# Two-layer hybrid encoder: weight splits leave GpSimd, native tiles read the residual itself

## Chip, cores and metric

The kernel runs on one core of one Trainium2 chip. The metric is device time in microseconds (us) of one execution; lower is better. The engines are TensorE (PE in the profile, its weight loads PEld), VectorE (DVE), ScalarE (ACT), GpSimd (POOL) and SyncE (SP, which issues the DMAs).

## The reference

Two layers run over 592 tokens at once: 16 meta tokens, 512 prompt tokens and 64 tokens of a running stream; the model width is 1024. Everything is float32.

```python
for l in range(2):
    h = h + 0.5 * swiglu(rms(h, ln_ffa_w[l]), wg, wu, wd)    # 1024 -> 2816 -> 1024
    h = h + mixer(rms(h, ln_mix_w[l]))                       # Mamba-2 SSD heads and HGRN2 heads
    h = h + 0.5 * swiglu(rms(h, ln_ffb_w[l]), wg, wu, wd)
y = rms(h, ln_f_w)
# rms(x, w) = x * rsqrt(mean(x * x) + 1e-6) * w      swiglu(x) = (silu(x @ wg) * (x @ wu)) @ wd
```

So there are four feed-forward blocks with the same shapes, and two mixers. Each block reads 34.6 MB of weights, once.

## The kernel before

The residual `h` is kept transposed in SBUF: 8 tiles (`m` or `k`) of 128 features by 592 tokens, worked on as two halves of 296 tokens.

**Split products.** Most products are made of float32r parts: a weight is rounded to a high part `wh` (float32r) and the rest is the low part `wl`; the activation likewise (`gh`, `gl` or `qh`, `ql`). Three products are summed: high by high, high by low, low by high (L578 to L580, and L607 to L609 in a quad). `convert` makes the parts of one weight unit of 128 x (4 x 128): the high part (L518 on ScalarE or L520 on GpSimd), then the low part (L524, on VectorE or GpSimd).

**A feed-forward block** has 22 tiles of 128 hidden features. The first two (`NPLAIN`, the native ones) are multiplied as plain float32 (`job.whole`, L571). They do not wait for the norm's statistics: the input is `h` times the norm's weight, in a tile `nh` made by `Norm.parts`, and the result is multiplied by the reciprocal root mean square `rstd` afterwards, in the sinks `gate` and `up` (L919 to L944). While TensorE runs these four jobs (two gates, two ups), the statistics become ready and `Norm.combine` builds the normed input of the remaining 20 tiles: for each of 4 `j` a pair `x1`, `x2` (L762), sums and differences of its halves in `y` and `x1` (L764 to L766), one more combination after the first split (L773), and `split` makes the parts `qh` (ScalarE, L792) and `ql` (VectorE, L794) of four combinations `p`.

**A quad** is one of the 20 tiles: gate and up together as seven multiplications of half-size blocks (a Strassen-like scheme), each of 4 x 3 products, 84 in all. Its weights need four sums (`combine`, L502) of the four raw tiles, and seven conversions. The sinks of the seven multiplications evict partial sums (ScalarE L858, L864, L868; VectorE L872 to L891); three of the multiplications start only after the eviction of an earlier one (`gates`), since they add to the same sum. `u` is one of these evicted sums (L864 on ScalarE, L877 on VectorE).

**Down products** follow after 6, 6, 5 and 5 tiles and add to `h` (L964). The mixer projects with the same split products, and runs its scans on all engines.

**Buffers.** `bT` holds 50 tiles of 592 columns, `braw` 6 raw weight tiles, `bhi` and `blo` 6 high and 6 low parts, `bzq` 4 tiles that the weight sums use.

**Order.** Every chain is a generator that yields (engine, duration, what it waits for, buffers it needs). `Plan.run` simulates time, always takes the task with the earliest start, then the lowest rank, and the instructions are issued in that order; each engine executes its own in that order. The rank is mostly the place of the job in the list of jobs (`near(order)`). Where a task names two engines, the planner takes the one that ends first by its cost formulas. `hops` are the costs it adds for handing over.

```python
        t = yield (S, G), (ns_act(n), 700 + 0.95 * n), (*waits, prev) if prev else waits, (bhi,)
        ...
        t = yield (V, G), (ns_dve(n), ns_pool(n)), (t,), (blo,)
```

`chain` makes the high parts take their buffers in the order of the jobs. Raw weight tiles are fetched in the order of the jobs by one generator (`fetch`), as `braw` has room; a native tile keeps its raw buffers until its second half has been multiplied.

Of the kernel before, what the change touches and what calls it, by code (L numbers as in the profile page):

```python
# [9 lines left out]
F32 = mybir.dt.float32  # L10
# [104 lines left out]
def ns_dve(n):  # L115
    return 157 + n / 0.96


def ns_act(n):
    return 205 + n / 1.2  # L120
# [6 lines left out]
class Plan:  # L127
    def __init__(self, hops):

        self.hops = hops  # L130
        self.tasks, self.busy, self.seq = [], {}, 0
# [10 lines left out]
    def start(self, req, behind):  # L142
# [49 lines left out]
def body(ctx: ExitStack, tc: tile.TileContext, a: dict, o: dict):  # L192
# [7 lines left out]
    plan = Plan({PE: (200.0, 60.0), V: (130.0, 0.0), S: (150.0, 0.0), G: (100.0, 0.0)})  # L200
# [199 lines left out]
    class Job:  # L400
# [5 lines left out]
        def __init__(self, name, src, ks, x, ev, hvs, sink, rank=1, few=0, after=None, whole=False, late=False):  # L406
# [37 lines left out]
    def fetch():  # L444
# [9 lines left out]
        for i, job in enumerate(jobs):  # L454
# [4 lines left out]
            for k0, k1, u in job.units:  # L459
                t = yield "DMA", 190 * (k1 - k0), (), (braw,)  # L460
# [3 lines left out]
                if job.whole:  # L464
                    u.hi = raw
                    u.ready.set(t)
                elif job.few:
# [3 lines left out]
                if i == 0:  # L471
                    for b, g in ((0, 1), (1, 1), (2, 1)) if k0 == 0 else ():
                        yield from fetch_x(b, g)
            if i == 1:
# [5 lines left out]
                load_params()  # L480

# [25 lines left out]
    def convert(u, raw, chain, done, *waits):  # L507
# [4 lines left out]
        t = yield (S, G), (ns_act(n), 700 + 0.95 * n), (*waits, prev) if prev else waits, (bhi,)  # L512
# [4 lines left out]
        if plan.pick == 0:  # L517
            S.activation(hi, raw, AF.Copy)  # L518
        else:
            G.tensor_scalar(hi, raw, 1.0, 0.0, op0=ALU.mult, op1=ALU.add)  # L520
# [20 lines left out]
    def products():  # L541
# [12 lines left out]
        for job, hv, ks in steps:  # L554
# [29 lines left out]
            if hf == job.hvs[-1][0]:  # L584
                if job.whole:
                    braw.put(t, len(job.units))
                else:
                    bhi.put(t, len(job.units))
# [85 lines left out]
    class Norm:  # L674

        def __init__(self, key, l, name, whole=False):
# [1242 lines left out]
```

## Time and profile before

| | us |
|---|---|
| median of 3 runs | 2409.16 (2406.61 to 2411.24) |
| the profiled execution | 2411.44 |
| its span, first to last instruction | 2409.7 |
| TensorE busy | 2333.8 |
| VectorE busy | 1747.8 |
| ScalarE busy | 980.6 |
| GpSimd busy | 627.7 |

The profile is of one execution. Busy times are unions of intervals; matmuls overlap in the pipeline, so their listed durations are longer than the time from one to the next. The next VectorE or ScalarE instruction also starts shortly before the listed end of the one ahead of it. The granted clock is 1.00 at 2.4 GHz and 0.50 at 1.2 GHz, as a mean over the stretch.

### The profile page before, as it was taken

The numbers are of one execution on the slowest core, as the hardware profiler recorded it, in microseconds if no ns is written. First come the engines' busy times: TensorE is split into PE (matmuls) and PEld (weight loads), VectorE is DVE, ScalarE is ACT, GpSimd is POOL, SyncE is SP. The second block draws the span as 40 slices with busy tenths as digits, with TensorE's granted clock in tenths as the row PEclk, the third lists the DMA queues.
The fourth block names the chain that finished last, engine by engine and source line by source line (L and its number), as shares of the span: only waits on it lengthen the run. The fifth ranks groups of instructions, "written<-read, shape, count | busy, mean of one in ns | idle before, by whom it ended". The sixth has DMA issues, their size and how long they took to land. (4 is left out here: it accounts for less than half of the span.)

```text
span 2409.7 us, 43335 instructions
## 1 busy us (share of the span) xinstructions
PE 2333.8 (97%) x16703; PEld 2262.8 (94%) x16703; DVE 1747.8 (73%) x3130; ACT 980.6 (41%) x1987; POOL 627.7 (26%) x630
## 2 busy tenths in 40 slices
PE   7999999999999899999989999999999998999998
PEld 6899999998889799999979999999988997999998
DVE  6866667687986776676677667676889768685775
ACT  5434334334444443343544344352353543353443
POOL 4322212243422223121222212123334114110012
PEclk9899999999999999999999999999999999999999
DMA  4222332331112123323222332323311122323232
GB/s 127 75 84 88 89 92 78 95 83 44 39 47 74 53 80 88 90 80 94 80 70 79 88 88 82 90 83 89 80 50 36 51 62 70 96 85 92 80 99 73
DMA packets 370366, 188.27 MB, mean 78 GB/s; under 512 B 16672, under 2 KB 367696, under 8 KB 370160
## 3 DMA queue, kind: packets, MB, share of 16 engines
q1 hardware_dynamic: 370160, 185.50, 26.9%
q8 instruction: 132, 2.16, 0.4%
q14 instruction: 74, 0.61, 0.1%
HBM read 180.94 MB, written 4.51 MB: 77 GB/s over the span
## 5 line engine op out<-in xcount | busy, mean ns | idle before, releaser
L578 PE MATMUL pd<-gh,wh 128*128 128x296 f32 (+3 forms) x1408 | 419.6, 298 | 0.3 <-ACT gh L895 0.3
L579 PE MATMUL pd<-gl,wh 128*128 128x296 f32 (+3 forms) x1408 | 419.4, 298 | 0.4 <-DVE gl L897 0.4
L580 PE MATMUL pd<-gh,wl 128*128 128x296 f32 (+3 forms) x1408 | 419.4, 298 | 0.0
L518 ACT ACTIVATE wh<-wr 128x512 fp32r<-128x512 f32 (+2 forms) x461 | 263.0, 571 | 371.3 <-PE pd L579 236.7
L524 DVE TENSOR_TENSOR wl<-wr,wh 128x512 fp32r<-128x512 f32 (+2 forms) x503 | 336.3, 686 | 45.2 <-ACT wh L518 42.0
L607 PE MATMUL pq<-qh_a,wh 128*128 128x296 f32 x1120 | 341.0, 304 | 10.8 <-DVE u L877 6.0
L608 PE MATMUL pq<-ql_a,wh 128*128 128x296 f32 x1120 | 339.0, 303 | 12.3 <-DVE ql_a L794 12.3
L608 PE MATMUL pq<-ql_b,wh 128*128 128x296 f32 (+1 forms) x1120 | 336.2, 300 | 12.2 <-DVE ql_b L794 12.2
L607 PE MATMUL pq<-qh_b,wh 128*128 128x296 f32 (+1 forms) x1120 | 335.8, 300 | 6.1 <-DVE u L877 5.1
L609 PE MATMUL pq<-qh_a,wl 128*128 128x296 f32 x1120 | 338.0, 302 | 1.9 <-POOL wl L524 1.9
L609 PE MATMUL pq<-qh_b,wl 128*128 128x296 f32 (+1 forms) x1120 | 335.2, 299 | 0.0
L520 POOL TENSOR_SCALAR wh<-wr 128x512 fp32r<-128x512 f32 (+1 forms) x179 | 130.2, 728 | 726.2 <-PE pd L579 172.9
L524 POOL TENSOR_TENSOR wl<-wr,wh 128x512 fp32r<-128x512 f32 (+2 forms) x137 | 197.5, 1444 | 400.9 <-ACT wh L518 386.1
L518 ACT ACTIVATE wh<-ws 128x512 fp32r<-128x512 f32 x293 | 184.7, 631 | 282.9 <-PE pq L608 137.9
L964 DVE SCALAR_TENSOR_TENSOR h<-pd,h 128x296 f32<-128x296 f32 (+3 forms) x256 | 117.5, 463 | 205.7 <-PE pd L580 204.3
L579 PEld LDWEIGHTS pd<-gl,wh 128*128 128x128 f32 x1408 | 265.1, 188 | 0.6 <-DVE gl L897 0.6
L578 PEld LDWEIGHTS pd<-gh,wh 128*128 128x128 f32 x1408 | 264.9, 188 | 0.6 <-ACT gh L895 0.6
L580 PEld LDWEIGHTS pd<-gh,wl 128*128 128x128 f32 x1408 | 264.8, 188 | 0.0
L607 PEld LDWEIGHTS pq<-qh_a,wh 128*128 128x128 f32 x1120 | 214.0, 191 | 16.5 <-issue 7.8
L608 PEld LDWEIGHTS pq<-ql_a,wh 128*128 128x128 f32 x1120 | 214.1, 191 | 14.9 <-DVE ql_a L794 14.8
L608 PEld LDWEIGHTS pq<-ql_b,wh 128*128 128x128 f32 x1120 | 212.8, 190 | 14.3 <-DVE ql_b L794 14.2
L607 PEld LDWEIGHTS pq<-qh_b,wh 128*128 128x128 f32 x1120 | 213.0, 190 | 9.5 <-issue 4.2
(437 smaller groups left out, 5210.4 us busy)
## 6 DMA issues: line engine op xcount, KB each, us to landing
wr<-in_w_in SPq DMA_DIRECT2D x112, 256.0 KB, 3.1
wr<-in_ffa_w_gate SPq DMA_DIRECT2D x88, 256.0 KB, 3.0
wr<-in_ffa_w_up SPq DMA_DIRECT2D x88, 256.0 KB, 3.1
wr<-in_ffb_w_gate SPq DMA_DIRECT2D x88, 256.0 KB, 3.0
wr<-in_ffb_w_up SPq DMA_DIRECT2D x88, 256.0 KB, 3.1
wr<-in_ffa_w_down SPq DMA_DIRECT2D x96, 192.0 KB, 2.6
wr<-in_ffb_w_down SPq DMA_DIRECT2D x96, 192.0 KB, 2.6
wr<-in_w_out SPq DMA_DIRECT2D x32, 256.0 KB, 3.0
```

Source lines behind the costliest of these rows:

```text
L518: S.activation(hi, raw, AF.Copy)
L520: G.tensor_scalar(hi, raw, 1.0, 0.0, op0=ALU.mult, op1=ALU.add)
L524: (V, G)[plan.pick].tensor_tensor(u.lo[:, :u.n], raw, hi.bitcast(F32), op=ALU.subtract)
L578: PE.matmul(out[:, :n], u.hi[:, i], xh, start=(j == 0), stop=False)
L579: PE.matmul(out[:, :n], u.hi[:, i], xl, start=False, stop=False)
L580: PE.matmul(out[:, :n], u.lo[:, i], xh, start=False, stop=(j == nk - 1))
L607: PE.matmul(out, u.hi[:, j], xh, start=(new and j == 0), stop=False, skip_group_check=True)
L608: PE.matmul(out, u.hi[:, j], xl, start=False, stop=False, skip_group_check=True)
L609: PE.matmul(out, u.lo[:, j], xh, start=False, stop=(j == UK - 1), skip_group_check=True)
L964: V.scalar_tensor_tensor(h[:, m, sl], pt, 0.5, h[:, m, sl], op0=ALU.mult, op1=ALU.add)
```

## The change

- `convert` makes every high part on ScalarE and every low part on VectorE; GpSimd makes none.
- The native tiles multiply `h` itself (`Norm.x`), and the norm's weight goes on the matrix: the raw unit is loaded straight into a `bhi` buffer (`whole`), and VectorE multiplies it there by the column of norm weights, broadcast over the 128 columns (`scaled`). `Norm.parts` makes no tile `nh` for these norms, and 8 `bT` tiles are not taken.
- Native units take no `braw` buffer; they queue in `chain` with the high parts for `bhi`. Only the first job's are fetched inside `fetch`; the other ones are tasks of their own.
- The fourth combination's high and low part share one `bT` tile (before, two `j` shared two tiles). `x1`, `x2` and `y` are each given back when their own last reader is done, not all together.
- The planner's costs and handovers change, and it is told that GpSimd and VectorE block one another (`shared`), which it applies where a task may choose between engines.

```diff
 def ns_dve(n):
-    return 157 + n / 0.96
+    return 67 + n / 0.96
 def ns_act(n):
-    return 205 + n / 1.2
+    return 90 + n / 1.2
...
             at = max(ready + self.hops.get(e, (0.0, 0.0))[1], self.busy.get(e, 0.0))
+            if len(eng) > 1 and e in self.shared:
+                at = max(at, self.busy.get(self.shared[e], 0.0))
...
             self.busy[eng] = end
+            if isinstance(req[0], tuple) and eng in self.shared:
+                self.busy[self.shared[eng]] = end
...
-    plan = Plan({PE: (200.0, 60.0), V: (130.0, 0.0), S: (150.0, 0.0), G: (100.0, 0.0)})
+    plan = Plan({PE: (200.0, 60.0), V: (220.0, 0.0), S: (265.0, 0.0), G: (100.0, 0.0)}, {G: V})
...
             for k0, k1, u in job.units:
+                if job.whole:
+                    if i == 0:
+                        yield from whole(i, job, src, k0, k1, u, chain)
+                    else:
+                        plan.add(near(job.order), whole(i, job, src, k0, k1, u, chain))
...
+                    continue
                 t = yield "DMA", 190 * (k1 - k0), (), (braw,)
...
-                if job.whole:
-                    u.hi = raw
-                    u.ready.set(t)
...
+    def whole(i, job, src, k0, k1, u, chain):
+        prev, chain[0] = chain[0], Ev()
+        mine = chain[0]
+        t = yield "DMA", 190 * u.n, (prev,) if prev else (), (bhi,)
+        u.hi = bhi.tile(f"wr{i}", dtype=F32)
+        SP.dma_start(u.hi[:, :u.n], src[:, k0:k1])
+        mine.set(0.0)
+        plan.add(near(job.order), scaled(job.whole, k0, k1, u, t + 2000.0))
+
+    def scaled(norm, k0, k1, u, t):
+        t = yield V, ns_dve(u.n * P), (t, col_ev[norm.key])
+        w = col[norm.key][:, 8 * norm.l + k0:8 * norm.l + k1].rearrange("p (k o) -> p k o", o=1)
+        V.tensor_tensor(u.hi[:, :u.n], u.hi[:, :u.n], w.to_broadcast([P, u.n, P]), op=ALU.mult)
+        u.ready.set(t)
...
-        t = yield (S, G), (ns_act(n), 700 + 0.95 * n), (*waits, prev) if prev else waits, (bhi,)
+        t = yield S, ns_act(n), (*waits, prev) if prev else waits, (bhi,)
...
-        t = yield (V, G), (ns_dve(n), ns_pool(n)), (t,), (blo,)
+        t = yield V, ns_dve(n), (t,), (blo,)
         u.lo = blo.tile("wl")
-        (V, G)[plan.pick].tensor_tensor(u.lo[:, :u.n], raw, hi.bitcast(F32), op=ALU.subtract)
+        V.tensor_tensor(u.lo[:, :u.n], raw, hi.bitcast(F32), op=ALU.subtract)
...
-                if job.whole:
-                    braw.put(t, len(job.units))
-                else:
-                    bhi.put(t, len(job.units))
+                bhi.put(t, len(job.units))
+                if not job.whole:
                     blo.put(t, len(job.units))
...
         def x(self, k, sl):
-            return self.hi[k][:, sl] if self.whole else (self.hi[k][:, sl], self.lo[k][:, sl])
+            return h[:, k, sl] if self.whole else (self.hi[k][:, sl], self.lo[k][:, sl])
...
+            if self.whole:
+                t = yield "none", 0, ts
+                self.ev[m][hf].set(t)
+                return
...
-            yield "none", 0, (e4, ends[1], ends[2])
-            bT.put(max(e4.t, ends[1].t, ends[2].t), 3)
+            yield "none", 0, (t, ends[2])
+            bT.put(max(t, ends[2].t))
+            yield "none", 0, (e4,)
+            bT.put(e4.t)
...
-            if p < 3 or j % 2 == 0:
-                t = yield S, ns_act(n), (t,), (bT, bT)
-                dst = self.q[p, j] = [bT.tile(f"q{c}_{self.name}", dtype=F32R) for c in "hl"]
...
+            t = yield S, ns_act(n), (t,), (bT, bT) if p < 3 else (bT,)
+            dst = self.q[p, j] = [bT.tile(f"q{c}_{self.name}", dtype=F32R) for c in ("hl" if p < 3 else "4")]
+            qh, ql = (d[:, :n] for d in dst) if p < 3 else (dst[0][:, :n], dst[0][:, n:2 * n])
```

## Rows read from the trace of the kernel before

**Rows 1.** The page's busy times of the engines, with share of the span and instructions.

```profile
PE 2333.8 (97%) x16703; PEld 2262.8 (94%) x16703; DVE 1747.8 (73%) x3130; ACT 980.6 (41%) x1987; POOL 627.7 (26%) x630
```

**Rows 2.** Windows by stage: start:end, length, busy us of each engine, granted clock, DMA.

```profile
120.00:540.00 420.00, 417.57 (x3050) 414.63 (x3049) 290.88 (x501) 155.22 (x305) 112.40 (x132) 1.00 0.31 87
540.00:700.00 160.00, 149.54 (x1131) 139.23 (x1129) 137.35 (x289) 68.88 (x168) 56.58 (x43) 0.97 0.16 45
...
880.00:1240.00 360.00, 356.97 (x2541) 350.36 (x2541) 236.54 (x407) 140.80 (x270) 78.84 (x74) 1.00 0.29 84
1240.00:1320.00 80.00, 71.89 (x466) 67.89 (x465) 67.13 (x105) 34.66 (x66) 24.63 (x18) 0.96 0.28 81
1320.00:1640.00 320.00, 316.58 (x2313) 314.14 (x2312) 220.61 (x373) 126.42 (x243) 78.55 (x75) 1.00 0.30 88
...
1740.00:1900.00 160.00, 151.84 (x1148) 141.59 (x1146) 136.12 (x281) 68.75 (x167) 54.19 (x45) 0.97 0.16 44
```

**Rows 3.** TensorE's waits over the span (us, times, longest), then of 1240 to 1320.

```profile
PE pq L608 <- DVE ql_a L794: 12.3, 8, 3.9
PE pq L608 <- DVE ql_b L794: 12.2, 7, 4.2
PE pq L607 <- DVE u L877: 11.1, 24, 1.3
...
PE pq L607 <- ACT u L864: 5.6, 9, 3.3
...
PE pq L607 <- DVE u L877: 1.1, 1, 1.1
```

**Rows 4.** Windows of first quads: from their first product to their last.

```profile
48.40:74.40 26.00, 18.30 (x86) 15.96 (x85) 25.14 (x33) 8.33 (x18) 16.35 (x10) 0.67 0.20 59
...
1252.15:1272.90 20.75, 14.28 (x86) 13.74 (x85) 19.82 (x26) 6.49 (x14) 11.82 (x8) 0.84 0.25 74
2018.90:2040.40 21.50, 15.61 (x87) 14.29 (x86) 21.50 (x26) 6.79 (x16) 14.49 (x11) 0.76 0.25 71
```

**Rows 5.** Instructions of the two split lines, min/median/max ns, forms of the shown ones.

```profile
L520 POOL TENSOR_SCALAR wh<-wr x179: 395/621/1727, 39.2 to 2386.0; 128x512 fp32r<-128x512 f32 x139, 128x256 fp32r<-128x256 f32 x40
L520 POOL TENSOR_SCALAR wh<-ws x27: 617/621/1137, 144.0 to 2303.9; 128x512 fp32r<-128x512 f32 x27
...
L524 DVE TENSOR_TENSOR wl<-ws,wh x233: 675/685/1814, 72.3 to 2351.7; 128x512 fp32r<-128x512 f32 x117
L524 POOL TENSOR_TENSOR wl<-wr,wh x137: 1032/1391/1935, 40.1 to 2344.1; 128x512 fp32r<-128x512 f32 x105, 128x384 fp32r<-128x384 f32 x16, 128x256 fp32r<-128x256 f32 x16
L524 POOL TENSOR_TENSOR wl<-ws,wh x87: 1273/1503/3626, 50.2 to 2049.1; 128x512 fp32r<-128x512 f32 x87
```

**Rows 6.** ScalarE's groups by form: busy us, mean ns, idle before.

```profile
L518 ACT ACTIVATE wh<-ws 128x512 fp32r<-128x512 f32 x293 | 184.7, 631 | 282.9 <-PE pq L608 137.9 <-DVE ws L502 87.0 <-PE pd L579 48.2
...
L720 ACT ACTIVATE nh_b<-h,par_b 128x296 f32<-128x296 f32 x16 | 8.7, 541 | 9.9 <-DVE h L1781 9.9
```

**Rows 7.** VectorE's timeline in the third block: start, us, instruction.

```profile
1229.10 1.57 DVE L762 SCALAR_TENSOR_TENSOR x_a<-h,par_a,rs_a 128x592 f32<-128x592 f32 x2
1230.71 0.47 DVE L764 TENSOR_TENSOR y_a<-x_a,x_a 128x296 f32<-128x296 f32 x1
...
1243.59 0.76 DVE L794 TENSOR_TENSOR ql_a<-x_a,qh_a 128x592 fp32r<-128x592 f32 x1
...
1258.37 1.83 DVE L794 TENSOR_TENSOR ql_a<-y_a,qh_a 128x592 fp32r<-128x592 f32 x1
...
1272.00 1.78 DVE L502 TENSOR_TENSOR ws<-wr,wr 128x512 f32<-128x512 f32 x1
```

**Rows 8.** Sum of the windows 1228.7 to 1252.15 and 1252.15 to 1268.9.

```profile
sum 40.20, PE 33.73 PEld 27.63 DVE 39.18 ACT 16.47 POOL 12.74; mean PE 16.87 PEld 13.82 DVE 19.59 ACT 8.23 POOL 6.37
```

**Rows 9.** SP's timeline before the third block.

```profile
1226.11 2.90 SPq L462 DMA_DIRECT2D wr<-in_ffa_w_up  x2
```

**Rows 10.** GpSimd's timeline in the first mixer.

```profile
582.51 7.40 POOL L1433 TENSOR_TENSOR st_o<-st_o,mhalf 128x4 f32<-128x4 f32 x2 [5.06 <-DVE st_o L1430]
```

More of the change, by code (lines that the diff above doesn't have):

```diff
@@ L127, with __init__ @@
 class Plan:
-    def __init__(self, hops):
-        self.hops = hops
+    def __init__(self, hops, shared):
+        self.hops, self.shared = hops, shared
         self.tasks, self.busy, self.seq = [], {}, 0
@@ L400, in body, with __init__ @@
     class Job:
-        def __init__(self, name, src, ks, x, ev, hvs, sink, rank=1, few=0, after=None, whole=False, late=False):
+        def __init__(self, name, src, ks, x, ev, hvs, sink, rank=1, few=0, after=None, whole=None, late=False):
             self.rank, self.few, self.after, self.whole, self.late = rank, few, after, whole, late
@@ L459, in fetch @@
             for k0, k1, u in job.units:
+                if job.whole:
[3 more added lines that the diff above has]
+                        plan.add(near(job.order), whole(i, job, src, k0, k1, u, chain))
+                    if i == 0:
+                        for b, g in ((0, 1), (1, 1), (2, 1)) if k0 == 0 else ():
+                            yield from fetch_x(b, g)
+                    continue
                 t = yield "DMA", 190 * (k1 - k0), (), (braw,)
@@ L691, in put @@
         def put(self, t):
-            bT.put(t, KD if self.whole else 2 * KD)
+            bT.put(t, 2 * KD)
         def start(self):
@@ L704, in feed, with parts @@
             yield from self.parts(m, hf, sl, *ts, sooner=1e3)
-        def parts(self, m, hf, sl, *ts, sooner=0.0, later=0.0):
+        def parts(self, m, hf, sl, *ts, sooner=0.0):
             n = sl.stop - sl.start
-            t = yield (G, S), (ns_pool(n) - 200 + sooner, ns_act(n) + 90 + later), \
-                (*ts, col_ev[self.key], *((self.made[m],) if hf else ())), () if hf else (bT,) * (1 if self.whole else 2)
+            if self.whole:
+                t = yield "none", 0, ts
+                self.ev[m][hf].set(t)
+                return
+            t = yield (G, S), (ns_pool(n) - 200 + sooner, ns_act(n) + 90), \
+                (*ts, col_ev[self.key], *((self.made[m],) if hf else ())), () if hf else (bT, bT)
             if hf == 0:
-                self.hi[m] = bT.tile(f"nh_{self.name}", dtype=F32 if self.whole else F32R)
-                if not self.whole:
-                    self.lo[m] = bT.tile(f"nl_{self.name}", dtype=F32R)
+                self.hi[m] = bT.tile(f"nh_{self.name}", dtype=F32R)
+                self.lo[m] = bT.tile(f"nl_{self.name}", dtype=F32R)
                 self.made[m].set(0.0)
@@ L720, in parts @@
                 S.activation(hi, h[:, m, sl], AF.Copy, scale=w)
-            if not self.whole:
-                t = yield V, ns_dve(n) + 60, (t,)
-                V.scalar_tensor_tensor(self.lo[m][:, sl], h[:, m, sl], w, hi.bitcast(F32), op0=ALU.mult, op1=ALU.subtract)
+            t = yield V, ns_dve(n) + 60, (t,)
+            V.scalar_tensor_tensor(self.lo[m][:, sl], h[:, m, sl], w, hi.bitcast(F32), op0=ALU.mult, op1=ALU.subtract)
             self.ev[m][hf].set(t)
@@ L741, in qx @@
             p, half = self.PAIRS[name]
+            n, q = self.n, self.q[p, j]
             if p == 3:
-                half = j % 2
-            sl = slice(half * self.n, (half + 1) * self.n)
-            return tuple(v[:, sl] for v in self.q[p, j])
+                return q[0][:, 0:n], q[0][:, n:2 * n]
+            return tuple(v[:, half * n:(half + 1) * n] for v in q)
         def qx_ev(self, name, j):
@@ L842, in feed @@
             self.start()
-            yield from self.parts(m, hf, sl, *ts, later=1e3 * hf)
+            yield from self.parts(m, hf, sl, *ts)
     def gated(q, g, s0):
@@ L948, in ffn @@
                 if f < NPLAIN:
-                    jobs.append(Job(f"g{f}_", wg[:, fs], range(KD), norm.x, norm.x_ev, hvs, gate, whole=True))
-                    jobs.append(Job(f"u{f}_", wu[:, fs], range(KD), norm.x, norm.x_ev, hvs, up,
-                                    after=norm.put if f == NPLAIN - 1 else None, whole=True))
+                    jobs.append(Job(f"g{f}_", wg[:, fs], range(KD), norm.x, norm.x_ev, hvs, gate, whole=norm))
+                    jobs.append(Job(f"u{f}_", wu[:, fs], range(KD), norm.x, norm.x_ev, hvs, up, whole=norm))
                     continue
```

21 lines of the change are left out of this document (4 added, 17 removed).

## The prediction

> **What bounds the kernel now.** I read the page first, then the windows by stage, then TensorE's waits, then the timelines of one stage in which it waits. The page says that TensorE is busy in 2333.8 of 2409.7 us [rows 1], so all the other engines together can give back at most its 76 us of idle time and what the clock loses behind it. The windows say where that is [rows 2]. In the long stretch of quads and down products (120 to 540 us) TensorE misses only 2.4 of 420 us, and runs 3050 instructions in 417.6 us, 0.137 us each. At each start of a feed-forward block it misses about 8 of 80 us (1240 to 1320 stands for the four), and the granted clock is 0.96, so some 3 us more go there. The two mixers miss 10.5 and 8.2 us. The waits name the cause [rows 3]: 24.5 us are for `ql`, the low parts of the combined inputs that the first quad of a block reads, written by VectorE; 16.7 us are for the two gates `u` inside the quads.
>
> The four first quads are 84 products each, 84 x 0.137 = 11.5 us if nothing is late. They took 26.0 us in the first block, 20.75 in the second and third (the row of the third stands), and 21.5 in the last [rows 4]: 14.5, 9.2, 9.2 and 10.0 us too long, 43 us together, more than half of all that can be won. In them VectorE is busy nearly without a break (25.1 of 26.0, 19.8 of 20.75), GpSimd for 11.8 to 16.4 us, ScalarE for a third; the granted clock is 0.67 to 0.84, so part of the time goes at the 1.2 GHz level after a wait.
>
> **What the change does, and its costs.** *The splits leave GpSimd.* Today it makes 179 + 27 = 206 high parts and 137 + 87 = 224 low parts [rows 5]. A low part of 128x512 is 1.39 to 1.50 us there, 0.68 on VectorE when nothing disturbs it, and the next VectorE instruction then starts 0.08 before its end, so 0.60. A high part is 0.63 on ScalarE [rows 6], by the same reading 0.54. So VectorE gets at most 224 x 0.60 = 134 us more work and ScalarE at most 206 x 0.54 = 111 us; ScalarE is at 41% [rows 1] and stays under half.
>
> What VectorE gets back is the stretch. Follow the third block, whose statistics are ready at 1228.7 us [rows 7]. A `ql` of 592 columns takes 0.76 us while GpSimd is idle (1243.59) and 1.83 us while GpSimd subtracts (1258.37). Counted with undisturbed slots (0.69 for 592 columns, 0.60 for 512, 0.39 for 296, 1.49 for a pair `x1`, `x2`), VectorE's work from 1228.7 to its last `ql` at 1268.9 is: four pairs 6.0, twelve half-width combinations with their handover 5.3, twelve `ql` 8.3, four L773 and four half `ql` 3.0, fifteen plain sinks 5.7, four weight sums and one low part 3.0, one gate sum 0.4: 31.7 us. It was busy for 39.2 us, with GpSimd busy for 12.7 [rows 8]. The difference, 7.5 us, is the stretch: 0.59 us per busy us of GpSimd. A low part there thus costs VectorE some 0.59 x 1.45 = 0.86 us, more than the 0.60 of doing it itself.
>
> The same rows against a rule: the Trainium skill, SBUF — State Buffer, section "SBUF: two separate sides", says that VectorE instructions with two SBUF inputs and GpSimd exclude one another for a whole instruction. By it all 12.7 us would come back in such a stage instead of 7.5, some 5 us more in each of four, and the sum would be near 48 instead of 28; the trace shows the smaller figure, and I keep to it.
>
> *The norm's weights go on the matrices.* Per block 8 units of 128x512 are multiplied on VectorE, 32 x 0.60 = 19 us in all; an operation of this form is not in the trace, and its bounds are the 0.60 of the same-sized subtraction undisturbed and 1.83 of the slowest disturbed one; GpSimd is quiet there, so 0.60. The multiply needs only a weight and a column of parameters, no activations. With six `whi` buffers the units of the first gate, the first up and the second gate land before or around the block's start, where VectorE still waits for the statistics; only the last up's two units must wait until the first gate's products have freed theirs. Today too SP issues that gate's successor at 1226.11, when the buffers come free [rows 9]; the multiplies then stand in VectorE's queue ahead of the combinations: 1.2 us of work, and up to 0.4 us more each if the transfer lands later than planned. Behind them wait the pairs, and behind those TensorE. In exchange 64 scaled copies of the residual go (8 tiles, 2 halves, 4 blocks), 0.54 us each on ScalarE [rows 6]; TensorE waited for none of them, so this is worth 0.
>
> *Raw buffers for the quads.* The six raw buffers no longer hold the native weights, so the four raw tiles of a block's first quad can land earlier and its four weight sums (2.4 us) can be made before the statistics are ready, in VectorE's idle time. If the order does not use that, the gain from it is 0. The quads' high parts now share the six `whi` buffers with eight native units; the first two come free after the second of four native jobs, so four can be converted before the quads begin, and the other three while those four run (4 x 12 x 0.137 = 6.6 us for 3 x 0.6 of VectorE). I put no cost on it; its cover is that 6.6 us, and without it each late unit costs some 1.3 us (a high and a low part in a row).
>
> *The fourth combination in one tile, earlier release of `x1`, `x2`, `y`, the planner's new constants:* same instructions and same number of buffers, no price by themselves. The constants reorder queues, which is inside the range.
>
> **The sum.** In the block at 1228.7 VectorE's work becomes 31.7 + 7 x 0.60 (GpSimd's low parts) + 1.2 = 37.1 us, or 34.7 with the sums made ahead, against 40.2 elapsed: ready 3.1 to 5.5 us earlier. The last unit of the quad needs 1.6 us on TensorE and some 0.5 of handover after that, so the quad ends at 1265.5 to 1267.9 and not at 1272.9: 5.0 to 7.4 us. If the remaining waits again leave the clock at its lower level (0.16 of 20.75 us), 3.3 less, so 1.7 to 7.4. I take 5.5, near the middle of the undisturbed case, since fewer and shorter waits are left. Three such blocks: 16.5 (5 to 22). The first block lost 14.5 instead of 9.2 us by the same cause; in proportion 8.6, of which I take 7 (3 to 9.6). Second quads: each waits some 1.1 us for `u` [rows 3] while VectorE's sums take 1.78 instead of 0.68 us beside GpSimd [rows 7]; three like it, worth 2 in all (0 to 5). Steady quads: 2.4, 3.0 and 3.4 us of waits, 8.8 in three stretches [rows 2], mostly for `u` behind VectorE; ScalarE gets busier, so 1 (-5 to 6). Mixers: GpSimd's 36 splits there leave VectorE and ScalarE, but the largest wait hangs on the two powers on GpSimd that took 7.40 us together [rows 10] while VectorE ran without a break, and those stay: 1 (-4 to 5). Beginning of the kernel: the first products need no scaled copy, 0.5 (0 to 1.5). Sum 28 us. The profiled execution is 2411.4 us (span 2409.7, 1.7 around it), so it would be 2383.4; the median of the runs shown is 2.3 lower, 2409.2, so **2381**. All lower bounds together cancel (2410), all upper ones give 49 us (2360); the forecast's own range is 2360 to 2400.
>
> **Rivals.**
>
> *VectorE becomes the longer bound (slower).* Place: the first quads, where it is busy for 95% of the time. If the stretch is not given back (it is DMA or queueing and not GpSimd), the seven low parts and two multiplies add 9 x 0.60 = 5.4 us to each stage: 4 x 5.4 = 21.6, 2431 us. It decides from a stretch of 0.60 us per low part downwards; 0.76 against 1.83 us for one shape, with and without GpSimd beside it, speaks against it [rows 7]. Chance 0.10, of which 0.03 ends within the bound. The Trainium skill, Perfetto Trace Analysis, "Optimizing Scalar/DVE Operations", would send work of a saturated VectorE elsewhere, GpSimd included, though it doubts that this pair helps; read by its first half alone, this rival is its case.
>
> *ScalarE's queue makes the gates late.* Place: 76 later quads. The gates' three evictions run on ScalarE, which now makes all seven high parts; each can find one of 0.63 us ahead of it. With one gate per quad late by 0.35 us, 76 x 0.35 = 27 us, the gain is gone (2408); at 0.5 us it is slower (2419). Only 5.6 us of waits are for ScalarE's `u` today [rows 3], and it is busy 155 of 420 us [rows 2]; both speak against it. Chance 0.08, 0.05 slower and 0.03 within the bound.
>
> *Hidden anyway.* VectorE is ready 3 us earlier, but the waits keep the clock low, or the multiplies and sums come in the wrong order: 1.7 x 3 + 2, about 2402. Chance 0.10, of which 0.02 within the bound.
>
> **Numbers.** The forecast has 0.72. What a measurement of this kernel can tell from no change is about 0.2%, 5 us. Faster 0.72 + 0.08 = 0.80, same 0.03 + 0.03 + 0.02 = 0.08, slower 0.07 + 0.05 = 0.12. The range 2357 to 2408 leaves out the slower cases and half of the unchanged ones, 0.16, and some 0.03 below.
>
> **What would show it.** Right: no split on GpSimd; VectorE's `ql` and `wl` of one shape all near their undisturbed 0.77 and 0.68; its busy time down in spite of more instructions; first quads of 13 to 16 us; the granted clock in them above 0.84; waits for `ql` under 10 us in all. Wrong: first quads as long as now, with VectorE still busy without a break; new waits of TensorE for ScalarE's `u` or for `wh`; weights waiting on `whi` buffers; longer mixers.

## The result, and the profile after

The changed kernel takes 2346.97 us (median, 2345.73 to 2350.83), the kernel before 2410.2 us beside it (2406.61 to 2411.29): ratio 0.9743, 95% interval 0.9726 to 0.976. That is 34 us below the forecast of 2381 and outside its range. The profiled execution took 2345.73 us, its span is 2343.6. The page's busy times, against [rows 1]:

```profile
PE 2307.6 (98%) x16703; PEld 2243.3 (96%) x16703; DVE 1703.8 (73%) x3391; ACT 1083.8 (46%) x2155; POOL 122.0 (5%) x167
```

VectorE runs 261 instructions more in 44 us less. TensorE's idle time fell from 76 to 36 us, and its busy time fell by 26 us at the same 16703 instructions; both come back to this below. VectorE's groups by form after the change (busy us, mean ns, idle before) show means at the undisturbed length for splits and weight sums (before: 802, 724 and 888 ns for the same three groups, with single ones of up to 1814 ns in [rows 5]):

```profile
L546 DVE TENSOR_TENSOR wl<-wr,wh 128x512 fp32r<-128x512 f32 x384 | 261.6, 695 | 29.6 <-ACT wh L542 24.0
L546 DVE TENSOR_TENSOR wl<-ws,wh 128x512 fp32r<-128x512 f32 x320 | 216.9, 685 | 50.0 <-ACT wh L542 47.2
L527 DVE TENSOR_TENSOR ws<-wr,wr 128x512 f32<-128x512 f32 x160 | 109.5, 684 | 28.3 <-DMA wr<-in_ffb_w_up 15.8 <-DMA wr<-in_ffa_w_up 11.6
```

The four first quads, in windows from their first product to their last (compare [rows 4]):

```profile
53.75:67.08 13.33, 12.70 (x86) 11.69 (x85) 13.30 (x26) 5.91 (x14) 0.00 (x0) 1.00 0.14 41
...
1219.41:1232.82 13.41, 12.70 (x86) 11.68 (x85) 13.41 (x26) 5.53 (x13) 0.00 (x0) 1.00 0.13 39
1963.76:1977.48 13.72, 12.49 (x86) 11.45 (x85) 13.72 (x28) 5.54 (x13) 0.00 (x0) 1.00 0.13 38
sum 53.88, PE 50.62 PEld 46.52 DVE 53.85 ACT 22.50 POOL 0.00; mean PE 12.66 PEld 11.63 DVE 13.46 ACT 5.63 POOL 0.00
```

No GpSimd, a granted clock of 1.00, and lengths 1.8 to 2.2 us above the 11.5 us of 84 undisturbed products. The first of them begins at 53.75 instead of 48.37 us: something was lost ahead of it. TensorE's waits of the whole span (us, times, longest), against [rows 3]:

```profile
PE pS L1640 <- DVE xw L1598: 6.7, 2, 3.3
PE xT L358 <- DMA x<-in_x_prompt: 5.8, 3, 4.4
PE pu L593 <- DVE sh_a L665: 3.9, 1, 3.9
PE yT L1695 <- DVE y_t L1690: 3.5, 3, 1.5
PE pd L600 <- ACT gh L913: 2.4, 2, 2.0
PE pq L628 <- DVE ql_b L812: 1.9, 2, 1.2
PE pq L628 <- DVE ql_a L812: 1.3, 2, 0.7
PE pq L627 <- DVE u L895: 1.1, 2, 0.9
```

The waits for `ql` fell from 24.5 to 3.2 us, those for `u` from 16.7 to 1.1 us, with none left for ScalarE's `u`; one of 3.9 us at the beginning is new.

Where the time came from is seen when the span is cut at the first and last products of each stage, read from TensorE's timeline (us; "rest" is a block's quads and down products after its first quad, "other" the output products and native tiles; the 6.2 us of the span behind the last product are left out). The third, fourth and last columns are experiments told below; the last is the fastest kernel found.

| stage | before | same order, GpSimd free | splits only | after | costs by stage |
|---|---|---|---|---|---|
| to the first quad | 48.4 | 46.9 | 48.2 | 53.8 | 47.6 |
| four first quads | 89.0 | 81.0 | 69.6 | 53.9 | 56.9 |
| four rests | 1473.0 | 1451.4 | 1450.9 | 1450.2 | 1450.8 |
| two mixers | 586.9 | 571.4 | 565.0 | 573.9 | 564.1 |
| other | 206.3 | 206.1 | 206.3 | 205.6 | 205.6 |

The forecast had 23.5 us in the first quads (35.1 came), 3 in the rests (22.8), 1 in the mixers (12.9), 0.5 at the beginning (-5.4 came). The sums of the windows of the four rests and of the two mixers, before:

```profile
sum 1472.98, PE 1455.25 PEld 1445.81 DVE 1020.17 ACT 601.50 POOL 327.39; mean PE 363.81 PEld 361.45 DVE 255.04 ACT 150.38 POOL 81.85
...
sum 586.85, PE 568.23 PEld 543.31 DVE 463.37 ACT 237.28 POOL 196.04; mean PE 284.11 PEld 271.65 DVE 231.68 ACT 118.64 POOL 98.02
```

and after:

```profile
sum 1450.20, PE 1445.14 PEld 1441.22 DVE 1017.85 ACT 675.57 POOL 14.77; mean PE 361.29 PEld 360.31 DVE 254.46 ACT 168.89 POOL 3.69
...
sum 573.92, PE 562.28 PEld 538.33 DVE 433.98 ACT 281.12 POOL 98.33; mean PE 281.14 PEld 269.17 DVE 216.99 ACT 140.56 POOL 49.16
```

More than half of GpSimd's splitting lay in the rests, where the forecast saw almost nothing to win.

### The profile page after: what moved, and what is told of

It reads as the page before. It is cut to its first block, busy times and chain, and to the rows that moved or that the text cites. A ratio compares the mean times of both kernels' runs of the same rounds, so it can differ in the third digit from the quotient of the medians.

```text
span 2343.6 us, 42925 instructions
## 1 busy us (share of the span) xinstructions
PE 2307.6 (98%) x16703; PEld 2243.3 (96%) x16703; DVE 1703.8 (73%) x3391; ACT 1083.8 (46%) x2155; POOL 122.0 (5%) x167
## 4 chain that ended last, share of the span: by engine, by line
PE 83%; DVE 12%; DMA 2%; ACT 1%; issue 1%; SPq 0%; POOL 0%; DVEq 0%; ACTq 0%
PE pq L629 11%; PE pq L627 11%; PE pq L628 11%; PE pd L601 8%; PE pd L602 8%; PE pd L600 8%; DVE wl L546 2%; PE pg L593 2%; PE px L601 1%; PE px L600 1%; PE px L602 1%; PE po L600 1%; PE pa L1320 1%; PE po L601 1%; PE po L602 1%; DVE ws L527 1%
## 5 line engine op out<-in xcount | busy, mean ns | idle before, releaser
L542 ACT ACTIVATE wh<-wr 128x512 fp32r<-128x512 f32 (+2 forms) x640 | 365.4, 574 | 416.4 <-PE pd L601 242.4
L546 DVE TENSOR_TENSOR wl<-wr,wh 128x512 fp32r<-128x512 f32 (+2 forms) x640 | 388.0, 624 | 59.9 <-ACT wh L542 52.6
L628 PE MATMUL pq<-ql_a,wh 128*128 128x296 f32 x960 | 287.4, 299 | 1.3 <-DVE ql_a L812 1.3
L628 PE MATMUL pq<-ql_b,wh 128*128 128x296 f32 (+1 forms) x960 | 285.8, 298 | 1.9 <-DVE ql_b L812 1.9
L627 PE MATMUL pq<-qh_a,wh 128*128 128x296 f32 x960 | 287.5, 299 | 0.1
L629 PE MATMUL pq<-qh_a,wl 128*128 128x296 f32 x960 | 286.2, 298 | 0.2
L627 PE MATMUL pq<-qh_b,wh 128*128 128x296 f32 (+1 forms) x960 | 285.3, 297 | 0.1
L546 DVE TENSOR_TENSOR wl<-ws,wh 128x512 fp32r<-128x512 f32 x320 | 216.9, 685 | 50.0 <-ACT wh L542 47.2
L629 PEld LDWEIGHTS pq<-qh_a,wl 128*128 128x128 f32 x960 | 180.8, 188 | 0.7 <-DVE wl L546 0.7
L629 PEld LDWEIGHTS pq<-qh_b,wl 128*128 128x128 f32 x960 | 180.5, 188 | 0.8 <-DVE wl L546 0.8
```

The costliest lines, as they stand in the source:

```text
L546: V.tensor_tensor(u.lo[:, :u.n], raw, hi.bitcast(F32), op=ALU.subtract)
L627: PE.matmul(out, u.hi[:, j], xh, start=(new and j == 0), stop=False, skip_group_check=True)
L628: PE.matmul(out, u.hi[:, j], xl, start=False, stop=False, skip_group_check=True)
L629: PE.matmul(out, u.lo[:, j], xh, start=False, stop=(j == UK - 1), skip_group_check=True)
```

## Experiments

The kernel before ran beside each group of runs, with medians of 2409.2, 2410.6, 2403.8 and 2406.4 us, so kernels of different groups are compared by ratio, and stages by their own times.

**1. The splits alone, and the rest alone.** On the kernel before, only the splits' engines are changed:

```diff
-        t = yield (S, G), (ns_act(n), 700 + 0.95 * n), (*waits, prev) if prev else waits, (bhi,)
+        t = yield S, ns_act(n), (*waits, prev) if prev else waits, (bhi,)
...
-        t = yield (V, G), (ns_dve(n), ns_pool(n)), (t,), (blo,)
+        t = yield V, ns_dve(n), (t,), (blo,)
```

> The kernel before with one edit: every high part on ScalarE, every low part on VectorE; planner constants and native tiles as before. Theory A (GpSimd's splits slow VectorE, and that is where the time was, in the later quads and mixers too): 45 to 55 of the 63 us come, about 2360, and TensorE's waits for VectorE's u shrink from 11 us to under 3. Theory B (the new planner constants put the queues in a better order, and the later quads and mixers gained from that): only the first quads gain, 20 to 25 us, about 2387, and u keeps most of its 11 us. Theory C (the native tiles and the freed raw buffers gave it): 15 us or less.

Measured: 2347.78 us, 0.9746 (0.9731 to 0.976), the whole gain and more than theory A had. The waits for VectorE's `u` are 2.0 us, as it said; in the first quads TensorE now waits 11.4 us for `wl`. The other part alone is the kernel after with these lines and the planner's numbers put back:

> The other part of the change alone: native tiles read the residual itself with the norm's weights on the matrix, and the raw buffers are kept for the quads; the splits may still go to GpSimd, with the planner's numbers of before. Theory, GpSimd beside VectorE is what costs the 62 us: GpSimd makes some 400 parts again, is busy for 500 to 620 us, first quads again take about 20 us, and the time is 2395 to 2412. Rival, the buffers and the smaller load at the starts of the blocks are worth much by themselves and only add up with the other part to little: 2355 to 2385.

Measured: 2408.46 us, 0.9992 (0.9981 to 1.0002), no change. The rival, that the buffers are worth much by themselves, falls.

**2. GpSimd allowed again in the kernel after** (the two lines above reversed, the `shared` rule kept), **and the kernel after with the planner's old numbers and no `shared` rule.**

> The changed kernel with GpSimd allowed to split again, as the planner finds it best; new constants, blocking rule and native tiles stay. Theory A: loses in proportion to the splits that GpSimd makes, some 50 us if it makes 430 as before, under 10 if the rule leaves it fewer than 80. Theory B and C: within 5 us of the changed kernel, 2347.

Measured: 2353.75 us, 0.9767 (0.9753 to 0.9782). The planner gave GpSimd three high parts and no low part (170 instructions, 125.6 us busy), so this did not test GpSimd beside VectorE; why it is 0.0024 slower than the kernel after was not followed.

> The changed kernel with the planner's old costs and handovers and without the blocking rule; splits on ScalarE and VectorE, native tiles on the residual. Theory A: 2347 to 2360, as the chip does the same work and only the order differs. Theory B: 30 to 40 us back, about 2382. Theory C: within 5 us of 2347.

Measured: 2346.56 us, 0.9744 (0.9728 to 0.976): the same total by another way. First quads 17.2, 17.0, 17.5 and 16.9 us (68.6 against 53.9), mixers 284.2 and 280.4 (564.5 against 573.9). So on the kernel with the native tiles the planner's numbers are worth 15 us in the first quads, and the same numbers cost the mixers 9 us. On the kernel before, the new numbers alone give no time: planning comes to a state in which no task can go on, with splits that want `bT` tiles and conversions that want `bhi` buffers.

**3. The order of before, with GpSimd free.** The planner decides as before; where it picked GpSimd, ScalarE or VectorE makes the part in that place:

```diff
-        if plan.pick == 0:
-            S.activation(hi, raw, AF.Copy)
-        else:
-            G.tensor_scalar(hi, raw, 1.0, 0.0, op0=ALU.mult, op1=ALU.add)
+        S.activation(hi, raw, AF.Copy)
...
-        (V, G)[plan.pick].tensor_tensor(u.lo[:, :u.n], raw, hi.bitcast(F32), op=ALU.subtract)
+        V.tensor_tensor(u.lo[:, :u.n], raw, hi.bitcast(F32), op=ALU.subtract)
```

> The kernel before with its own order, planner's numbers and buffers: at each place at which GpSimd made a high or a low part, ScalarE or VectorE makes it instead, in the same place of the order. So it tells the splits from the new order that the planner wrote for them. Theory, what counts is that GpSimd no longer reads beside VectorE and that its parts no longer come late: nearly all of the gain stays, 2345 to 2360, first quads 14 to 20 us. Rival, a good part of the 62 us came from the other order: 2365 to 2395.

Measured: 2366.57 us, 0.9847 (0.9832 to 0.9861), in the range of the rival: of the gain that the splits bring, some 37 us come in the order of before, and some 24 only with another order. The first quads, 23.4, 21.1, 18.8 and 17.6 us, are mostly longer than the theory's 14 to 20. Its busy times, and the sums of the windows of its first quads, rests and mixers:

```profile
PE 2322.9 (98%) x16703; PEld 2257.7 (96%) x16703; DVE 1698.6 (72%) x3354; ACT 1094.1 (46%) x2193; POOL 142.5 (6%) x200
```

```profile
sum 80.97, PE 66.87 PEld 59.54 DVE 73.76 ACT 31.62 POOL 0.00; mean PE 16.72 PEld 14.89 DVE 18.44 ACT 7.90 POOL 0.00
...
sum 1451.40, PE 1447.86 PEld 1445.60 DVE 1007.45 ACT 678.32 POOL 13.35; mean PE 361.96 PEld 361.40 DVE 251.86 ACT 169.58 POOL 3.34
...
sum 571.41, PE 561.31 PEld 536.90 DVE 440.00 ACT 266.01 POOL 100.18; mean PE 280.66 PEld 268.45 DVE 220.00 ACT 133.00 POOL 50.09
```

With not one instruction moved in the order, the rests lose 21.6 of the 22.8 us, and the mixers 15.4, more than the change kept; the first quads give only 8.0 of their 35.1. VectorE gained 224 low parts and lost 49 us of busy time. From there to the splits alone (the order that the planner writes when it has no GpSimd to count on) are another 11.4 us in the first quads and 6.4 in the mixers.

**4. GpSimd's parts made again for nobody.** The kernel of experiment 3, and at each place that was GpSimd's the same instruction into an unused tile; then a second form that holds none of the kernel's tiles (at the low parts' places only):

```diff
+        if plan.pick == 1:
+            G.tensor_scalar(junk[:, :u.n], raw[:, :, 0:124], 1.0, 0.0, op0=ALU.mult, op1=ALU.add)
...
+        if plan.pick == 1:
+            G.tensor_tensor(junk[:, :u.n], raw[:, :, 0:124], hi[:, :, 0:124].bitcast(F32), op=ALU.subtract)
```

```diff
+        if plan.pick == 1:
+            G.tensor_copy(spot, hi[:, 0, 0:1].bitcast(F32))
+            G.tensor_tensor(junk[:, :u.n], junk[:, :u.n], junk[:, :u.n], op=ALU.add)
```

> As the kernel with the same order and free GpSimd, and at each place at which GpSimd made a part it now makes it again into an unused tile (124 of 128 columns of each block, so 3% less), for which nobody waits: GpSimd has the load of before at the places of before, and VectorE and ScalarE do the real work. Theory A, the loss is the stretch of VectorE: 2395 to 2440, first quads of 20 to 28 us. Theory D, from the kernel with idle additions (14.5 us for 398 us of GpSimd): the stretch is worth 15 to 25 us over the kernel with the same order and free GpSimd, so 2362 to 2382, and the other 30 to 45 us of the change's gain were parts that GpSimd delivered late.

Measured: 2502.63 us, 1.0417 (1.0398 to 1.0436), far above both. Nobody waits for these parts, so GpSimd's work costs time without being late for anyone, and theory D's small price for the stretch falls. Its busy times and three of TensorE's waits:

```profile
PE 2364.2 (95%) x16703; PEld 2278.1 (91%) x16703; DVE 1902.8 (76%) x3354; ACT 1085.8 (43%) x2193; POOL 633.0 (25%) x630
```

```profile
PE pq L609 <- ACT u L866: 39.5, 34, 5.0
PE pq L609 <- DVE u L879: 21.0, 28, 3.5
PE pq L610 <- DVE ql_a L796: 20.7, 12, 5.1
```

VectorE: 204 us more for 490 us of GpSimd, 0.42 each. The 39.5 us for ScalarE's `u` may be another thing: a high tile that a late GpSimd still reads cannot be written again, and ScalarE stands in its queue. That is argued, not shown: of ScalarE's own listed waits only one, of 2.3 us, is for such a part. The second form leaves it out:

> As the kernel with GpSimd's parts made again for nobody, but without its hold on the kernel's buffers: only at the places of the low parts (224), a copy of one column of the high part, which sets the time, and then an addition of an unused tile to itself (128x496, two inputs), so that no raw or high tile waits for a slow GpSimd instruction. Theory, the 136 us that the echo cost came from VectorE's stretch: for about 310 us of additions 0.26 to 0.42 us of VectorE each, 80 to 130 us more busy time than 1699, and a time of 2385 to 2450. Rival, most of it came from tiles that a late GpSimd held, so that ScalarE could not write the next high part (TensorE waited 39.5 us for ScalarE's u there): the busy time rises as much, but the time is 2368 to 2385.

Measured: 2436.48 us, 1.0124 (1.0107 to 1.0141), inside the theory's range. Its busy times and two of its waits:

```profile
PE 2347.8 (96%) x16703; PEld 2266.3 (93%) x16703; DVE 1806.3 (74%) x3354; ACT 1087.7 (45%) x2193; POOL 517.0 (21%) x649
```

```profile
PE pq L611 <- DVE ql_a L797: 17.3, 12, 5.0
...
PE pq L610 <- ACT u L867: 7.9, 7, 3.2
```

375 us of GpSimd, some 274 of them additions, cost VectorE 108 us and the kernel 67 us by the ratios (0.9847 to 1.0124), about half of the echo's 137 (0.9847 to 1.0417). The first quads are 19 us longer than in experiment 3, the rests 39 and the mixers 13. So the stretch of VectorE is enough by itself for a loss of this size; that late parts cost nothing besides is not shown. The echo's other half came with a larger load and with tiles held, which are not told apart.

**5. What kind of GpSimd work it is.** On the kernel with the splits alone, after every third conversion, an addition of two inputs, or a copy of one column and three memsets, for nobody; and the kernel before with the low parts alone taken from GpSimd.

```diff
+            G.tensor_tensor(junk[:, :u.n], hi[:, :, 0:124].bitcast(F32), hi[:, :, 0:124].bitcast(F32), op=ALU.add)
```

> The splits on ScalarE and VectorE alone (2347.8 us), and beside them on GpSimd an addition for which nobody waits, after every third conversion (some 320 of them, 128x496 with two inputs, the sum goes to an unused tile). Nothing of the kernel's own work is on GpSimd that was not there. Theory A, a busy GpSimd that reads its inputs beside VectorE stretches VectorE: at 1.36 us each GpSimd gets 435 us more, at 0.37 to 0.59 us of VectorE for each that is 160 to 255 us more busy time of VectorE (1860 to 1955 instead of 1702), ql and wl take up to 1.8 us again, first quads 20 us or more, and the time is 2385 to 2440. Rival B, GpSimd's parts only came late (1.4 us instead of 0.68, and a handover from another engine): nobody waits for these, so VectorE's busy time stays within 20 us of 1702 and the time is 2347 to 2353.

```diff
+            G.tensor_copy(junk[:, 0, 0:1], hi[:, 0, 0:1].bitcast(F32))
+            for _ in range(3):
+                G.memset(junk[:, :u.n], 0.0)
```

> As the kernel with idle additions, but GpSimd only writes: after every third conversion a copy of one column and three memsets of the same unused tile (128x496), for which nobody waits. Theory A1, what excludes VectorE is GpSimd's reading of its inputs: VectorE's busy time stays within 40 us of 1702 and the time is 2347 to 2358, however long GpSimd is busy. Rival A2, any busy GpSimd stretches VectorE by its busy time, or it is GpSimd's writing: VectorE gets 0.37 to 0.59 us for each us that GpSimd is busy, and the time goes up with it as with the additions (per busy us of GpSimd the same loss).

> Half of the splits' edit: the low parts (two inputs) are VectorE's alone, the high parts (one input, converted) may still go to GpSimd, 150 to 250 of them at 0.7 to 0.8 us. Theory, a GpSimd instruction with two inputs is what VectorE is held by, and the low part is the late one of a unit: nearly all of the gain stays, 2348 to 2362. Rival, the high part comes first in every unit, so one that waits in GpSimd's queue makes its low part and the product late as well: 2370 to 2400.

The busy times with the additions,

```profile
PE 2315.6 (98%) x16703; PEld 2249.4 (95%) x16703; DVE 1805.3 (76%) x3354; ACT 1094.4 (46%) x2190; POOL 539.5 (23%) x523
```

with the memsets,

```profile
PE 2312.4 (98%) x16703; PEld 2251.2 (96%) x16703; DVE 1695.2 (72%) x3354; ACT 1093.0 (47%) x2190; POOL 773.3 (33%) x1483
```

and with only the low parts moved:

```profile
PE 2308.9 (98%) x16703; PEld 2248.9 (96%) x16703; DVE 1724.8 (74%) x3354; ACT 978.9 (42%) x1970; POOL 316.8 (14%) x423
```

The splits alone have VectorE at 1701.7 and GpSimd at 141.6. So 398 us of additions cost VectorE 104 us (0.26 each), 632 us of copies and memsets nothing (6 us less, as theory A1 said), 175 us of one-input conversions 23 us (0.13). Times: 2362.27 (0.9795, interval 0.9779 to 0.9811), 2348.49 (0.9741, 0.9724 to 0.9758) and 2345.61 us (0.9757, 0.9743 to 0.9772). The low parts alone bring all of the splits' gain, with 226 high parts still on GpSimd. The additions missed both forecasts: VectorE is stretched as theory A says, but less, and by the ratios (0.9746 to 0.9795) some 12 us of time follow, where 37 or more were expected. GpSimd is busy for only 12 us of the first quads here, and for 58.2 with the echo in its own tile: the planner of before put much of GpSimd's work where VectorE was fullest.

**6. The 5 us lost at the beginning.** SP's and TensorE's timelines of the kernel after show it:

```profile
12.17 0.38 SPq L513 DMA_DIRECT2D wr<-in_ffa_w_gate  x1
...
15.13 0.77 SPq L513 DMA_DIRECT2D wr<-in_ffa_w_up  x1
15.94 2.20 SPq L497 DMA_DIRECT2D wr<-in_ffa_w_up  x2
```

```profile
17.59 1.20 PE L593 MATMUL pg<-h,wr 128*128 128x296 f32 x4
22.68 1.82 PE L593 MATMUL pu<-h,wr 128*128 128x296 f32 x3 [3.90 <-DVE sh_a L665]
```

Six raw quad tiles (L513) go out before the weights of the second native product (L497), because `whole` of that job is now a task of the planner and no longer part of `fetch`. One condition puts it back:

```diff
-                    if i == 0:
+                    if i < 2:
                         yield from whole(i, job, src, k0, k1, u, chain)
```

> The kernel after, with one condition changed at the beginning: the weights of the second native product (the first up product, u0) are fetched in the fixed order, before the raw tiles of the first quads, as those of the first product are. Theory: the changed kernel lost 5.4 us up to its first quad because SP issued six raw quad tiles before those weights (TensorE waits 3.9 us at 22.68 us, first quad at 53.75 instead of 48.37). Then the first quad starts at 48 to 50 us, the wait of 3.9 us is gone and the time is 2341 to 2344. Rival, the delay comes from the multiplies by the norm's weights themselves (two 128x512 products on VectorE between the transfer and TensorE): the start stays above 52 us and the time at 2346 to 2349.

Measured: 2342.55 us, 0.9714 (0.97 to 0.9729); the first quad starts at 49.20, and the wait of 3.9 us is 1.0 us, now for the multiply by the norm's weights. Theory confirmed.

**7. The planner's numbers.** Three kernels from that of experiment 6: without the `shared` rule; with the new costs and the old handovers; and with the new numbers only while a feed-forward block is planned, those of before in the mixers (`COST` holds both sets, from which `ns_dve`, `ns_act` and the handovers are taken):

```diff
+            STAGE[0] = 0 if isinstance(job, Quad) or job.whole or job.name[0] == 'd' and job.name[1:-1].isdigit() else 1
+            plan.hops[V], plan.hops[S] = (COST[STAGE[0]][2], 0.0), (COST[STAGE[0]][3], 0.0)
```

> The kernel after with the second native product's weights fetched in the fixed order (2342.6 us), without the planner's rule that keeps GpSimd out while VectorE is busy; its new costs and handover times stay. Theory, the rule is what made the two mixers 5.3 and 3.7 us longer than with the splits alone (289.4 and 284.6 against 284.1 and 280.9): they go back to 284 to 286 and 280 to 282, the first quads stay at 13.4, and the time is 2333 to 2338. Rival, the new costs order the mixers worse: mixers as now, 2340 to 2346.

> The kernel after with the second native product's weights fetched in the fixed order, with the new costs of an instruction but the handover times of before (130 and 150 ns instead of 220 and 265). It tells the two apart. If the handover times made the first quads short: 16 to 18 us each and the mixers back to 284 and 281, 2340 to 2346. If the costs did: first quads 13 to 15, mixers as in the kernel after, 2340 to 2346 too; the stages decide, not the total.

> The kernel after with the second native product's weights fetched in the fixed order, and the planner's new costs and handover times only while a feed-forward block is planned; in the two mixers it plans with those of before. Theory, the new numbers win the first quads (13.4 us each against 17.2 with the old ones) and lose the mixers (289.4 and 284.6 against 284.2 and 280.4), each in its own place: first quads stay at 13 to 15, mixers go to 284 to 287 and 280 to 283, and the time is 2332 to 2338, the best of all. Rival, the losses in the mixers come from what the blocks leave behind (buffers, queues) and not from the numbers used in them: 2340 to 2346.

Without the rule: 2342.43 us, 0.9744 (0.973 to 0.9759), mixers 289.2 and 284.2; the rule is not it. Its first and last first quads, 16.4 and 15.2 us, are longer than expected. With the old handovers: 2347.52 us, 0.9756 (0.9742 to 0.9771), first quads 14.9, 13.4, 12.4 and 15.2, mixers 290.2 and 287.3; so the costs do both, though the time lies just above the 2340 to 2346 of either case. With costs by stage: **2331.45 us, 0.9689 (0.9675 to 0.9704)**, below the kernel after, as its theory said, though its first quad of 16.4 us is longer than expected (the others 13.4, 13.4 and 13.7). Against experiment 6 it is some 6 us by the ratios, whose intervals just touch, and 9 to 10 us by its mixers. The sums of the windows of its first quads and mixers:

```profile
sum 56.92, PE 52.60 PEld 48.03 DVE 56.26 ACT 23.02 POOL 0.00; mean PE 13.15 PEld 12.01 DVE 14.06 ACT 5.75 POOL 0.00
...
sum 564.08, PE 559.54 PEld 535.79 DVE 441.36 ACT 265.54 POOL 91.14; mean PE 279.77 PEld 267.90 DVE 220.68 ACT 132.77 POOL 45.57
```

## Why the prediction was wrong, and where it was right

**Right: the mechanism.** A low part on GpSimd costs VectorE more than making it would; experiments 1 and 3 show it for the kernel, 4 and 5 for GpSimd alone. Taken over the kernel the price is (49.2 + 224 x 0.60) / 485 = 0.38 us per busy us of GpSimd, not the 0.59 of the one stage it was read from. For the low parts alone experiment 5 gives it directly: VectorE took over 224 of them and was busy 23.0 us less (1747.8 to 1724.8), so each had cost it (23.0 + 224 x 0.60) / 224 = 0.70 us, less than the 0.86 forecast and more than the 0.60 of making it. In the third block VectorE's work ran from its first pair to the last `ql` piece in 33.8 us (1196.75 to 1230.58), just under the 34.7 forecast, the sums being made ahead:

```profile
1196.75 1.57 DVE L784 SCALAR_TENSOR_TENSOR x_a<-h,par_a,rs_a 128x592 f32<-128x592 f32 x2
1198.24 0.68 DVE L504 TENSOR_TENSOR wr<-wr,par_a 128x512 f32<-128x512 f32 x1
...
1229.38 1.20 DVE L812 TENSOR_TENSOR q_a<-x_a,q_a 128x296 fp32r<-128x296 f32 x3
```

The multiply by the norm's weights took 0.68 us, the slot of 0.60 that was counted. The rivals did not come: VectorE is full in the first quads, but they are 35 us shorter together, and the waits for ScalarE's `u` are gone.

**Mis-sized: the first quads**, 23.5 against 35.1 us. The argument followed one cause in a fixed order. With the order fixed that cause gives 8.0 us (experiment 3), at a granted clock of 0.71 to 0.82: about the case that the forecast had priced, 1.7 us for each of three blocks and 3 for the first, and set aside. The others are the order that the planner writes without GpSimd, 11.4, and, at the step "the constants reorder queues, which is inside the range", its new costs, 15 us (experiments 2 and 7). So the term was three times too large for its own cause, and that it looks too small is luck: two causes that it priced at nothing gave the rest.

**The step that failed: "Second quads ... 2" and "Steady quads ... 1".** All of the 16.7 us of waits for `u` in the forecast's own list [rows 3] lie in the four rests. It credited 3 us of them, and set against the others that ScalarE gets busier. No such loss came: ScalarE went from 41 to 46% busy, no wait after the change is for its `u`, and those for VectorE's `u` are 1.1 us. The rests gave 22.8 us, 21.6 of them from the splits in an unchanged order (experiment 3).

Read the sums of the rests again: TensorE's idle time fell from 17.7 to 5.1 us, and its busy time from 1455.3 to 1445.1 at the same clock of 1.00 and the same number of products but one. Part of that busy time was waiting, too. A product is listed as 0.30 us long, but the next one starts 0.135 us after it when nothing is late, so each wait is listed some 0.165 us short. Counted from start to start, the rests had 39 delays of more than 0.15 us beyond the usual 0.135, 24.1 us together; in experiment 3 there are 7 of 4.9 us, after the change 14 of 7.5 us. They make 19.2 of the 21.6 us of experiment 3 and 16.6 of the 22.8; what is left was not followed. And 314 us of GpSimd's splits took (12.7 + 156 x 0.60) = 106 us of VectorE's time in the rests (its busy time fell by 12.7 us in experiment 3 while it took over 156 low parts), a price that the forecast charged to the first quads alone.

**The step that failed in the mixers: "those stay: 1".** The forecast counted 36 splits of GpSimd in the mixers, but its two windows of 160 us [rows 2] cover little more than half of them: from first to last product, 295 and 292 us, there are 84, which kept GpSimd busy for 92 us. With those gone in the order of before (experiment 3) VectorE's busy time in the mixers fell from 463.4 to 440.0 us though it took over the low parts, and the mixers lost 15.4 us. Nor did the waits behind the powers stay: TensorE's wait for `yt`, 5.4 and 2.1 us in the two mixers, became 0.4 and 0.4. That is 6.7 of the 8.5 us by which its idle time fell; the other 6.9 us are busy time, with the granted clock up from 0.98 in both mixers to 0.99 and 1.00. Why the wait went is open. The powers did not become much shorter: the slow pair of each mixer took 6.4 us in experiment 3, against 7.4 and 6.5 before, and began some 1.5 and 1.2 us earlier in its mixer. In the kernel after they are shortest, and its mixers are yet longer than those of experiment 3. The power's group (busy us, mean ns) in experiment 3 and after, which had 2383 ns before:

```profile
L1430 POOL TENSOR_TENSOR st_o<-st_o,mhalf 128x4 f32<-128x4 f32 x8 | 15.6, 1956 | 184.7 <-DVE st_o L1427 184.7
...
L1450 POOL TENSOR_TENSOR st_o<-st_o,mhalf 128x4 f32<-128x4 f32 x8 | 10.1, 1263 | 162.0 <-DVE st_o L1447 162.0
```

The order that the planner writes without GpSimd gave 6.4 us more, and the new costs took 9 back.

**The sign was wrong at the beginning**, +0.5 against -5.4: of a step that was moved, SP's order of issue was not followed (experiment 6).

**The native tiles and raw buffers**, costed at nearly nothing, are nothing by themselves (0.9992). Whether they add to the new costs' 15 us is open: the new costs were measured only together with them, since on the kernel before they give none (experiment 2).

**The rule weighed beside the row.** By the Trainium skill, SBUF — State Buffer, section "SBUF: two separate sides", the forecast's sum would have been 48 by the prediction's estimate, nearer to the 63 measured. That nearness is no proof, as most of the 63 came from places that the sum priced at little or nothing. But the trace of the kernel before bears the rule out one instruction at a time. Of 92 `wl` and `ws` of 128x512 that VectorE began while GpSimd was making a low part of that shape, 81 ended 0.53 to 0.57 us after GpSimd's instruction, and the 92 took 1.48 us on average against 0.685 alone; the 64 that VectorE began first took 0.683, at most 0.693. The `ql` of 1258.37 [rows 7], which ended at 1260.20, stood behind this one, which ended at 1259.57:

```profile
1258.09 1.48 POOL L524 TENSOR_TENSOR wl<-wr,wh 128x512 fp32r<-128x512 f32 x1
```

Beside the memsets of experiment 5 nothing of this shows: 291 that VectorE began during one took 0.686 us, at most 0.697. So the 0.59 that the forecast kept to, and the 0.13 to 0.42 of the experiments, are no figures against the rule: they are averages over GpSimd's busy time, and an instruction that VectorE began first was not held.

## What to carry to other kernels

GpSimd next to a full VectorE is no spare engine: price each part there by what it takes from VectorE, over every stage in which it runs, and above all where VectorE is full. Do not write a listed wait off against a loss that no row shows, and count late starts as well: where products overlap, a wait is listed shorter than it is. Cut a stage at its first and last product before counting what runs in it. And numbers that plan one stage well can cost in another: here they were worth 15 us in one and minus 9 in the other, and using each in its place gave the fastest kernel measured.

## What the runs showed of the hardware that was not expected

- A `wl` or `ws` of 128x512 that VectorE begins during a low part on GpSimd ends some 0.55 us after it, however long that takes; one that it begins first is not slowed (0.683 against 0.685 us alone).
- GpSimd at 33% busy with memsets and copies of one column leaves VectorE untouched (1695.2 against 1701.7 us); at 23% with two-input additions it costs 104 us.
- 226 one-input conversions on GpSimd (175 us) cost 0.13 us of VectorE per us, about half of what the additions cost. One by one they hold VectorE in the same way: of 125 `wl` and `ws` of 128x512 that it began during one of 128x512, 112 ended 0.53 to 0.57 us after it.
- The same stretch of VectorE costs very unequal time: 104 us of it cost some 12 us in an order written for VectorE alone, 108 us cost some 67 in the order written with GpSimd's help. That the slack of the order makes the difference is argued, not shown.
